# Gate projections of a hybrid decoder layer: eight quarter products per pair of column blocks, or seven

## The chip, the cores and the metric

The kernel runs on one core of one Trainium2 chip. The metric is the device time of one execution in microseconds (us), median of several; lower is better. Everything is float32 at the borders of the kernel: inputs and the output.

Four engines matter here. TensorE (PE) multiplies and writes to PSUM. VectorE (DVE) and ScalarE (ACT) do elementwise work, and only they and PE reach PSUM. SyncE (SP) issues most DMA transfers, ACT and GpSimd (POOL) a few. Each engine works through its own list of instructions in order and waits where an operand, or the buffer for a result, isn't ready.

## What is computed

One layer of a decoder on 256 tokens with 2048 channels, cut to what matters:

```python
h = rms_norm(x, g_pre)
proj = h @ w_in                       # 2048 -> 17424 columns, 8192 of them are g_logits
(a_val, a_gate, sq, sk, sv, s_gate, cq, ck, cv, c_gate, c_lr, mq, m_gate, g_logits) = split(proj)
y_a = pool_mixer(a_val, a_gate, w_pool, pool_scale)          # causal pooling, 1024 wide
y_b = swa_mixer(sq, sk, sv, s_gate)                          # window attention, 512 wide
y_c = gla_mixer(cq, ck, cv, c_lr, c_gate, ...)               # gated linear attention, 1024 wide
y_m = mem_attn(mq, m_gate, mem, g_mem, w_mem_kv)             # attention into 256 memory tokens, 512 wide
gates = sigmoid(g_logits.reshape(B, S, 4, 2048) + b_merge)
merged = (gates[:, :, 0] * (y_a @ w_br_pool) + gates[:, :, 1] * (y_b @ w_br_swa)
          + gates[:, :, 2] * (y_c @ w_br_gla) + gates[:, :, 3] * (y_m @ w_br_mem))
out = x + rms_norm(merged @ w_out, g_post)
```

The gate projection is `h` (256 x 2048) times 16 blocks of weights (2048 x 512), one block for each branch `b` (0 pooling, 1 window, 2 linear, 3 memory) and each quarter `j` of the channels.

## The kernel before

**Precision by splitting.** Every large operand is split into a high and a low part in the format float32r, which PE multiplies in one pass: `hi = round(x)`, `lo = x - hi`. A product takes three matmuls: hi by hi, hi by lo, lo by hi. A weight unit of 1 MB comes into one of three `raw` buffers by an SP transfer (`load_raw`, L104). `split_w` (L110) then makes two halves of 1024 columns: ACT copies to `hi` (L113) and DVE subtracts (L114). There are five pairs of `hi` and `lo` buffers.

**Two forms of product.** `a_block` (L117) has the activations stationary and 512 weight columns moving: for each of its k slices of 128 channels and for both token tiles t, three matmuls (L133, L134, L135) into one of four PSUM banks of the tag `acc`. `b_unit` (L146) has the weights stationary and both parts of the activations moving: 16 times a matmul of 512 columns (L156) and one of 256 (L157), then a sum (L161, L162) and an `evac` function that multiplies by the row of 1/rms. The activations `h_at` are x times `g_pre`; 1/rms is applied behind each product, as a column (`xscol`) or a row (`xsrow`).

**Background work.** The small chains of the four mixers are generators in `queue`; `pull` takes one step of them between weight units. A scheduler then orders each engine's list, so that neighbours can swap; the tables of buffers set who waits for whom.

**Stages.** First x is loaded and split while the values `sv` of the window attention are computed (three `a_block`s from L278), then come the `b_unit`s of the window attention (28), the memory branch (12) and the linear attention (16), and then `merge` (L438) for each branch: memory, window, linear, and pooling last. `merge` computes for each quarter j the gate block (`a_block` over 16 slices, evacuated by L447 on DVE and the tanh of L448 on ACT into a tile of the tag `c2`), and behind it the branch projection (`a_block` over 4 or 8 slices), which L453, L455 and L456 multiply by the gate and add to `merged`. The pooling units (`av`, `ag`, 16) stand between the gates of memory and linear attention. The last `merge` also transposes `merged` (`transpose_block`, L695), and the output projection (`o0` to `o4`, L733 to L753), a norm and the residual follow.

The pieces at which the prediction looks are the branch ends, such as this one of before:

```python
                    vec.scalar_tensor_tensor(gates[t][:], gates[t][:], 1.0, a, op0=ALU.add, op1=ALU.mult)
                    vec.tensor_tensor(merged[t][:, js], merged[t][:, js], gates[t][:], op=ALU.add)
```

## Time and profile before

| what | value |
|---|---|
| time, median of 3 runs | 1184.74 us (1184.65 to 1184.75) |
| span of the profiled execution | 1182.7 us |
| between the span and the median | 2.0 us |
| PE, DVE, ACT, POOL busy | 1172.6, 715.9, 555.3, 13.8 us |
| granted TensorE clock, all stages | 1.00 |
| moved by DMA | 230.44 MB, mean 195 GB/s |
| first 8 us, 8 to 74 us: PE busy | 5.89, 65.78 us |
| 1170 us to the end: PE busy | 4.96 of 13.0 us |

The profiled execution has no time of its own beside its span; the 2.0 us to the median of the runs are what lies around it. A row of the timeline gives start, duration, engine, line, operation, output and inputs, and in brackets the idle time before it with its releaser. Durations of instructions on one engine overlap: the next one starts before the last one's results have landed. So what an instruction costs a full engine is the distance between two starts, and its duration is what a follower waits that needs the result.

### The profile page before, as it was taken

To read this page: it belongs to the slowest core of one execution; us is meant where nothing else is said; L and a number is where in the kernel's file an instruction comes from. 1 tells how busy PE (TensorE), PEld (TensorE's weight loads), DVE (VectorE), ACT (ScalarE), POOL (GpSimd) and SP (SyncE) were. 2 spreads that over 40 slices of the span, in tenths; PEclk is the share of its full clock that TensorE was granted. 3 is DMA by queue.
4 is the path that set the end of the run, shared out by engine and by line. 5 is a ranking of instruction groups with operands and counts; after the bars stand their busy time and mean duration, and the time that the engine had idled before them with its cause. 6 is when DMAs were issued, how large, how long until landed. Compare 5 with 4: busy or idle time off the path is not lost.

```text
span 1182.7 us, 15065 instructions
## 1 busy us (share of the span) xinstructions
PE 1172.6 (99%) x6014; PEld 1001.8 (85%) x6014; DVE 715.9 (61%) x943; ACT 555.3 (47%) x734; POOL 13.8 (1%) x36
## 2 busy tenths in 40 slices
PE   9999999999999999999999999999999999999997
PEld 7888888888888888899888888888888888888887
DVE  6656665664665555545856666777655555656454
ACT  7656444444554444345644444454444444444441
POOL 0000000000000000000000000000000000000000
PEclk9999999999999999999999999999999999999999
DMA  9867544544445555356444455555555555556642
GB/s 354 324 226 260 178 147 175 178 148 174 178 169 192 200 199 201 133 185 221 178 163 176 156 184 199 179 186 194 214 193 205 204 189 205 193 187 241 257 145 105
DMA packets 38838, 230.44 MB, mean 195 GB/s; under 512 B 4448, under 2 KB 4832, under 8 KB 14832
## 3 DMA queue, kind: packets, MB, share of 16 engines
q1 hardware_dynamic: 38048, 228.28, 54.5%
q10 hardware_dynamic: 720, 1.21, 0.3%
q8 instruction: 47, 0.77, 0.3%
q14 instruction: 23, 0.19, 0.0%
HBM read 227.37 MB, written 2.10 MB: 194 GB/s over the span
## 4 chain that ended last, share of the span: by engine, by line
PE 98%; issue 0%; DMA 0%; DVE 0%; ACT 0%; SPq 0%; DVEq 0%; POOLq 0%; POOL 0%
PE sp L341 1%; PE gmem0a L133 1%; PE gmem2a L133 1%; PE gmem1a L133 1%; PE gswa0a L135 1%; PE gmem2a L135 1%; PE gswa0a L133 1%; PE gmem0a L135 1%; PE gmem1a L135 1%; PE vma L135 1%; PE gmem2a L134 1%; PE gmem0a L134 1%; PE gpool1a L135 1%; PE o0a L135 1%; PE gmem1a L134 1%; PE vma L133 1%
## 5 line engine op out<-in xcount | busy, mean ns | idle before, releaser
L306 ACT ACTIVATE th<-xg 128x256 f32<-128x256 f32 x24 | 9.9, 411 | 18.1 <-DVE xg L304 18.1
L344 DVE SCALAR_TENSOR_TENSOR s<-big_cst,sp 128x128 f32<-128x128 f32 (+1 forms) x24 | 7.3, 349 | 3.5 <-PE sp L341 3.5
L341 PE MATMUL sp<-k,q 128*128 128x128 f32 (+1 forms) x48 | 9.1, 326 | 0.0
L349 ACT ACTIVATE s<-s,st 128x384 f32<-128x384 f32 (+1 forms) x8 | 6.2, 775 | 4.8 <-DVE st L348 4.8
L341 PEld LDWEIGHTS sp<-k,q 128*128 128x128 f32 x48 | 7.3, 190 | 0.8
L578 POOL TENSOR_TENSOR sq<-sq 128x256 f32<-128x256 f32 x4 | 3.4, 854 | 384.5 <-ACT sq L577 360.4
L179 ACT ACTIVATE xhl<-xr,vecs 128x256 fp32r<-128x256 f32 x16 | 6.9, 499 | 1.9 <-DMA xr<-in_xT 1.2
L704 ACT ACTIVATE mTh<-mtp 128x512 fp32r<-128x512 f32 x8 | 4.3, 596 | 6.5 <-PE mtp L702 6.5
L180 DVE SCALAR_TENSOR_TENSOR xhl<-xr,vecs,xhl 128x256 fp32r<-128x256 f32 x16 | 6.8, 482 | 0.7 <-ACT xhl L179 0.6
L367 PE MATMUL po<-pt,sv 128*128 128x256 f32 x24 | 7.2, 380 | 0.0
L179 ACT ACTIVATE mhl<-mr,vecs 128x256 fp32r<-128x256 f32 x16 | 7.0, 495 | 0.0
L180 DVE SCALAR_TENSOR_TENSOR mhl<-mr,vecs,mhl 128x256 fp32r<-128x256 f32 x16 | 6.9, 479 | 0.0
L759 DVE SCALAR_TENSOR_TENSOR yg<-yg,opart,xres 128x640 f32<-128x640 f32 (+2 forms) x8 | 5.5, 748 | 1.3 <-POOL opart L756 1.3
L348 DVE TENSOR_REDUCE st<-s 128x1 f32<-128x384 f32 (+1 forms) x8 | 6.0, 748 | 0.1
L726 ACT ACTIVATE oj<-o4a 128x256 f32<-128x256 f32 x2 | 0.8, 383 | 10.6 <-PE o4a L753 10.6
L362 ACT ACTIVATE pt<-tp 128x384 f32<-128x384 f32 x12 | 5.7, 477 | 0.0
L705 DVE SCALAR_TENSOR_TENSOR mTl<-mtp,mTh 128x512 fp32r<-128x512 f32 x8 | 5.2, 686 | 0.7 <-ACT mTh L704 0.4
L322 DVE TENSOR_TENSOR sqh<-sq,sqh 128x256 fp32r<-128x256 f32 x4 | 1.7, 424 | 5.9 <-ACT sqh L321 5.9
L456 DVE TENSOR_TENSOR merged<-merged,gmem 128x512 f32<-128x512 f32 x8 | 5.1, 684 | 0.0
L456 DVE TENSOR_TENSOR merged<-merged,ggla 128x512 f32<-128x512 f32 x8 | 5.1, 684 | 0.0
L456 DVE TENSOR_TENSOR merged<-merged,gpool 128x512 f32<-128x512 f32 x8 | 5.1, 684 | 0.0
L368 PEld LDWEIGHTS po<-pt,sv 128*128 128x128 f32 x24 | 4.6, 190 | 0.6
(3495 smaller groups left out, 4397.0 us busy)
## 6 DMA issues: line engine op xcount, KB each, us to landing
raw<-in_w_g SPq DMA_DIRECT2D x64, 1024.0 KB, 4.8
raw<-in_w_sqk SPq DMA_DIRECT2D x24, 1024.0 KB, 4.9
raw<-in_w_out SPq DMA_DIRECT2D x12, 1024.0 KB, 4.8
raw<-in_w_sv SPq DMA_DIRECT2D x8, 1024.0 KB, 7.7
raw<-in_w_cqk SPq DMA_DIRECT2D x8, 1024.0 KB, 4.8
raw<-in_w_cg SPq DMA_DIRECT2D x8, 1024.0 KB, 4.9
raw<-in_w_av SPq DMA_DIRECT2D x8, 1024.0 KB, 4.8
raw<-in_w_ag SPq DMA_DIRECT2D x8, 1024.0 KB, 4.9
```

The source lines that it names most:

```text
L133: ten.matmul(o, lhsT=sh[:, ts], rhs=hi[:, ws], start=(k == 0), stop=False)
L134: ten.matmul(o, lhsT=sh[:, ts], rhs=lo[:, ws], start=False, stop=False)
L135: ten.matmul(o, lhsT=sl[:, ts], rhs=hi[:, ws], start=False, stop=(k == nk - 1))
L179: act.activation(h, rawx[:, i, :], AF.Copy, scale=g[:, k : k + 1])
L180: vec.scalar_tensor_tensor(l, rawx[:, i, :], g[:, k : k + 1], h.bitcast(F32), op0=ALU.mult, op1=ALU.subtract)
L306: act.activation(th[:], xg[:], AF.Tanh, scale=0.5)
L341: ten.matmul(parts[g], lhsT=q3[:, g, it * P : (it + 1) * P], rhs=k3[:, g, :nj], start=True, stop=True)
L344: vec.scalar_tensor_tensor(s[:, g, :], dist[:, g, :], SLOPES[g * 4 + hh], parts[g], op0=ALU.mult, op1=ALU.add)
L348: vec.tensor_reduce(st[:, 0:1], s[:], axis=AX.XY, op=ALU.max, negate=True)
L349: act.activation(s[:], s[:], AF.Exp, bias=st[:, 0:1], accum_out=st[:, 1:2])
L367: ten.matmul(po[:], lhsT=sv[g][:, 0, vs], rhs=pt[g][:, 0:T], start=(g == 0), stop=False)
L456: vec.tensor_tensor(merged[t][:, js], merged[t][:, js], gates[t][:], op=ALU.add)
```

## The change

The gate projections are computed with seven quarter products instead of eight. For a pair of neighbouring column blocks j0, j1 of one branch, `h` is cut into four quarters (two token tiles by two halves of the channels) and the two weight blocks into four (two halves of the channels by two blocks). Sums and differences of quarters are multiplied in seven products instead of eight and put together again. The sums of activations (`quarter`, made once) are split into hi and lo; those of the weights are made on DVE for each of eight slices `kk` (L420, L421, L426) and split afterwards. The bias enters by a small matmul (`bias`).

For this, `h` is now normalised before it is split (`x_prep`), so that no product needs the 1/rms any more, and the memory branch's values `vm` are computed first, while x is prepared. The gates are no longer computed in `merge`: a generator `all_gates` is drawn on by `gates(work)`, which every `b_unit` and `a_block` calls with the PE time of the piece just issued; each step of the generator costs so much of a credit (0.8 for a half of a plain weight unit, 6.6 for a slice `kk` with sums). The finished gates (32 tiles of 128x512) are written to DRAM by ACT's queue and read back by SP's when the branch projections run, all of them at the end, quarter by quarter. The outputs of linear attention and pooling also wait in DRAM, over POOL's queue. PSUM is divided anew: the tag `seven` has four banks, `acc` two instead of four, `sm` two instead of four.

```diff
+GATE_SHARE = 1.07
...
     def sm(name, shape):
-        return ps.tile(shape, F32, tag="sm", bufs=4, name=name)
+        return ps.tile(shape, F32, tag="sm", bufs=2, name=name)
 
     def acc(name, shape):
-        return ps.tile(shape, F32, tag="acc", bufs=4, name=name)
+        return ps.tile(shape, F32, tag="acc", bufs=2, name=name)
+
+    def seven(name):
+        return ps.tile([P, 512], F32, tag="seven", bufs=4, name=name)
...
+    def gates(work):
+        if gate_stream[0] is None:
+            return
+        credit[0] += GATE_SHARE * work
+        while credit[0] > 0 and gate_stream[0] is not None:
+            try:
+                credit[0] -= next(gate_stream[0])
+            except StopIteration:
+                gate_stream[0] = None
...
+    def x_prep():
+        for c in range(4):
+            xn.append(c4(f"xn{c}", [P, 4, T]))
+            sync.dma_start(xn[c][:], ins["xT"][:, 4 * c : 4 * c + 4, :])
+            squares(xsq, xn[c], c)
+            for i in range(4):
+                k = 4 * c + i
+                act.activation(xn[c][:, i, :], xn[c][:, i, :], AF.Copy, scale=g_pre[:, k : k + 1])
+            yield
+        fold(xsq)
+        pr = sm("xpr", [P, T])
+        ten.matmul(pr[:], lhsT=ones[:], rhs=xsq[:, 0, 0], start=True, stop=True)
+        pool.memset(xsq[:, 1, 1], -0.5)
+        inv_rms(xrow, pr[:], xsq[:, 1, 1])
+        yield
+        for c in range(4):
+            for i in range(4):
+                vec.tensor_tensor(xn[c][:, i, :], xn[c][:, i, :], xrow, op=ALU.mult)
+            put_hilo(h_at.four(c, 0), h_at.four(c, 1), xn[c][:])
+            yield
...
+    def put_gate(b, j, t, src, dst):
+        act.activation(dst, src, AF.Tanh, scale=0.5)
+        gate_dram[b, j, t] = spill(f"gd{b}{j}{t}", [P, 512], F32)
+        act.dma_start(gate_dram[b, j, t][:], dst)
+
+    def gate_pair(b, jj):
+        j0, j1, n = 2 * jj, 2 * jj + 1, f"{b}{jj}"
+        w = ins["w_g"]
+        p1 = seven(f"p1{n}")
+        bias(p1[:], 4 * b + j0)
+        p1c = c2(f"p1c{n}", [P, 512])
+        for u in range(4):
+            raw = load_raw(w[b, j0, u], 2048)
+            for hf in range(2):
+                hi, lo = split_w(raw[:, hf * 1024 : (hf + 1) * 1024], 1024, f"gu{n}{u}{hf}")
+                for i in range(2):
+                    k = 4 * u + 2 * hf + i
+                    ws = slice(i * 512, (i + 1) * 512)
+                    mm3(p1[:], *tok(0, k), hi[:, ws], lo[:, ws], False, k % 8 == 7, k >= 8)
+                if u == 1 and hf == 1:
+                    act.activation(p1c[:], p1[:], AF.Copy)
+                yield 0.8
+        c11 = c2(f"c11{n}", [P, 512])
+        put_gate(b, j0, 0, p1[:], c11[:])
+        q4, q5, q6, q7 = [seven(f"q{i}{n}") for i in (4, 5, 6, 7)]
+        bias(q5[:], 16 + 2 * b + jj)
+        for kk in range(8):
+            raw = new_raw()
+            r4 = raw[:].rearrange("p (j u c) -> p j u c", j=2, u=2)
+            u, cs = kk // 4, slice((kk % 4) * 512, (kk % 4 + 1) * 512)
+            for j in range(2):
+                sync.dma_start(r4[:, j], w[b, j0 + j, u : u + 3 : 2, :, cs].rearrange("u p c -> p u c"))
+            vec.tensor_tensor(r4[:, :, 0, :], r4[:, :, 0, :], r4[:, 1, :, :], op=ALU.add)
+            vec.tensor_tensor(r4[:, 1, 1, :], r4[:, 1, 1, :], r4[:, 0, 0, :], op=ALU.add)
+            hi, lo = split_w(raw[:, 1024:2048], 1024, f"gt{n}{kk}a")
+            st, sp = kk == 0, kk == 7
+            mm3(q7[:], *quart(2, kk), hi[:, 0:512], lo[:, 0:512], st, sp)
+            mm3(q6[:], *quart(1, kk), hi[:, 512:1024], lo[:, 512:1024], st, sp)
+            vec.tensor_tensor(r4[:, 0, 1, :], r4[:, 0, 1, :], r4[:, 1, 1, :], op=ALU.add)
+            hi, lo = split_w(raw[:, 0:1024], 1024, f"gt{n}{kk}b")
+            mm3(q5[:], *quart(0, kk), hi[:, 0:512], lo[:, 0:512], False, sp)
+            mm3(q4[:], *tok(1, kk + 8), hi[:, 512:1024], lo[:, 512:1024], st, sp)
+            yield 6.6
+        v3, c21 = c2(f"v3{n}", [P, 512]), c2(f"c21{n}", [P, 512])
+        vec.tensor_tensor(p1c[:], q6[:], p1c[:], op=ALU.subtract)
+        vec.tensor_tensor(v3[:], q7[:], p1c[:], op=ALU.add)
+        vec.tensor_tensor(c21[:], q4[:], v3[:], op=ALU.subtract)
+        put_gate(b, j0, 1, c21[:], c21[:])
+        vec.tensor_tensor(v3[:], q5[:], v3[:], op=ALU.add)
+        put_gate(b, j1, 1, v3[:], v3[:])
+        vec.tensor_tensor(q5[:], q5[:], p1c[:], op=ALU.add)
+        for u in range(2, 4):
...
+                    mm3(q5[:], *quart(3, kk), hi[:, ws], lo[:, ws], False, kk == 7, True)
+                yield 0.8
+        put_gate(b, j1, 0, q5[:], c12[:])
...
+    for j in range(4):
+        merged[j] = c4(f"merged{j}", [P, 2, 512])
+        for i, (name, b, at, nky) in enumerate(branches):
+            a_block(f"b{name}{j}", [ins[f"w_br_{name}"][j, u] for u in range(nky // 4)], at, 512, br_evac(i, b, j))()
+        transpose_block(j)
```

Below, a "gate step" is one slice `kk` (its tiles are named `gt`), a "unit" is a `b_unit`, and `gu` and `gv` are the halves of plain gate weights ahead of and behind the eight steps of a pair. There are 8 pairs, so 64 gate steps, 64 `gu` halves and 32 `gv` halves.

How this moves instructions is shown at three places. The first is ACT's list near the start. In before, three blocks of `sv` follow each other and ACT does little but split their weights (`sv130h` and so on) and square x for the norm:

```order
L113 ACTIVATE sv130h<-raw_445 128x1024
L113 ACTIVATE sv131h<-raw_445 128x1024
L209 ACTIVATE xsx_447,xsssq<-xsx_447 128x1024
L243 ACTIVATE sv_107<-sv0a_111,xscol 128x512
L243 ACTIVATE sv_107<-sv0a_112,xscol 128x512
L113 ACTIVATE sv200h<-raw_497 128x1024
L113 ACTIVATE sv201h<-raw_497 128x1024
```

In the changed kernel the first block is `vm`, whose last four splits (`vm30h` to `vm33h`) stand among the preparation of the last chunk of the memory (`mhl`, `msq`) and of all four chunks of x (`xsq` squares, `xn` scaled by `g_pre`):

```order
L246 ACTIVATE xsq<-xn_275 128x1024
L319 ACTIVATE xn_275<-xn_275,vecs 128x256 x4
L246 ACTIVATE xsq<-xn_293 128x1024
L265 ACTIVATE mhl_96<-mr_302,vecs 128x256
L319 ACTIVATE xn_293<-xn_293,vecs 128x256 x4
L265 ACTIVATE mhl_96<-mr_302,vecs 128x256 x3
L246 ACTIVATE msq<-mr_302 128x1024
L138 ACTIVATE vm30h<-raw_301 128x512
L246 ACTIVATE xsq<-xn_328 128x1024
L138 ACTIVATE vm31h<-raw_301 128x512
L319 ACTIVATE xn_328<-xn_328,vecs 128x256 x4
L138 ACTIVATE vm32h<-raw_301 128x512
```

What moved: the squares and the scaling of x, which ran behind or beside three blocks, now stand ahead of the end of the first.

The second place is DVE's list in the middle, while the window attention's units run. One gate step (`gt115`, the raw buffer raw_6120) stands between the units `sq22` and `sk22`:

```order
L139 TENSOR_TENSOR sq220l<-raw_6058,sq220h 128x1024
L420 TENSOR_TENSOR raw_6120<-raw_6120 128x2x512
L139 TENSOR_TENSOR sq221l<-raw_6058,sq221h 128x1024
L421 TENSOR_TENSOR raw_6120<-raw_6120 128x512
L426 TENSOR_TENSOR raw_6120<-raw_6120 128x512
L139 TENSOR_TENSOR gt115al<-raw_6120,gt115ah 128x1024
L139 TENSOR_TENSOR gt115bl<-raw_6120,gt115bh 128x1024
L139 TENSOR_TENSOR sk220l<-raw_6147,sk220h 128x1024
L201 SCALAR_TENSOR_TENSOR q_5728<-sq22a,sq22s 128x256
L139 TENSOR_TENSOR sk221l<-raw_6147,sk221h 128x1024
```

In before, DVE had only the two splits of each unit there, a sum and a product by the row of 1/rms; the three additions and two more splits per step are new, and the product is gone.

The third place is PE's list at the end of a branch projection. In before, the gates' block `ggla1` follows the linear attention's branch block `bgla0`, with other PSUM tiles:

```order
L133 MATMUL bgla0a_7159<-bgla011h,yc_3836 128x512
L134 MATMUL bgla0a_7159<-bgla011l,yc_3836 128x512
L135 MATMUL bgla0a_7159<-bgla011h,yc_3837 128x512
L133 MATMUL ggla1a_7239<-ggla100h,xhl_91 128x512
L134 MATMUL ggla1a_7239<-ggla100l,xhl_91 128x512
```

In the changed kernel the next branch block `bpool0` follows, and with two `acc` banks in all its two tiles take the banks of `bgla0`:

```order
L144 MATMUL bgla0a_8591<-bgla011h,yc_8492 128x512
L145 MATMUL bgla0a_8591<-bgla011l,yc_8492 128x512
L146 MATMUL bgla0a_8591<-bgla011h,yc_8492 128x512
L144 MATMUL bpool0a_8668<-bpool000h,ya_8495 128x512
L145 MATMUL bpool0a_8668<-bpool000l,ya_8495 128x512
```

What moved: nothing stands between the last matmul of one branch block and the first of the next, and the next one writes where DVE still reads.

More of the change, by code (lines that the diff above doesn't have):

```diff
@@ L229 @@
-    x_chunk, h_at = make_T("x", ins["xT"], g_pre)
-    col, row, x_rstd = make_rstd("xs", ins["x"])
-    m_chunk, m_at = make_T("m", ins["memT"], g_mem)
-    mcol, mrow, m_rstd = make_rstd("ms", ins["mem"])
-    def run(gen):
-        for _ in gen:
-            pass
-    sv = [c4(f"sv{g}", [P, 2, 512]) for g in range(3)]
-    def sv_evac(j):
-        def evac(t, a):
-            act.activation(sv[j][:, t, :], a, AF.Copy, scale=col[:, t : t + 1])
-        return evac
-    first_x = x_chunk.load(0)
+        at.four = lambda c, i: hl[c][:, :, i, :]
@@ new lines, with m_put, m_norm @@
+    m_at = hilo_tiles("m")
+    msq = e8("msq", [P, 2, 4, T])
+    mrow = msq[:, 1, 0]
+    mcol = cst.tile([P, 2], F32, name="mcol")
+    def m_put(rawx, c, i):
+        k = 4 * c + i
+        h, l = m_at(k)
+        act.activation(h, rawx[:, i, :], AF.Copy, scale=g_mem[:, k : k + 1])
+        vec.scalar_tensor_tensor(l, rawx[:, i, :], g_mem[:, k : k + 1], h.bitcast(F32), op0=ALU.mult, op1=ALU.subtract)
+    def m_norm():
+        fold(msq)
+        pr = sm("mpr", [P, T])
+        ten.matmul(pr[:], lhsT=ones[:], rhs=msq[:, 0, 0], start=True, stop=True)
+        pc = sm("mpc", [P, 2, 2])
+        for t in range(2):
+            ten.matmul(pc[:, t, :], lhsT=msq[:, 0, 0, t * P : (t + 1) * P], rhs=ones[:, 0:2], start=True, stop=True)
+        pool.memset(msq[:, 1, 1], -0.5)
+        inv_rms(mrow, pr[:], msq[:, 1, 1])
+        inv_rms(mcol[:], pc[:, :, 0], half[:])
@@ L262, in load_first @@
         for i in range(4):
-            x_chunk.put(first_x, 0, i)
-        return raw
-    def mem_prep():
-        for c in range(4):
-            yield from m_chunk(c)
-        yield from m_rstd()
-    x_rstd_steps = x_rstd()
-    def load_second(u, src):
-        raw = load_raw(src, 2048)
-        next(x_rstd_steps)
-        return raw
-    sv_done = a_block("sv0", [ins["w_sv"][0, u] for u in range(4)], h_at, 512, sv_evac(0), load_first,
-                      lambda u: 1)
-    sv_done1 = a_block("sv1", [ins["w_sv"][1, u] for u in range(4)], h_at, 512, sv_evac(1), load_second)
@@ new lines, in quart, with tok, bias_prep @@
+    def quart(i, kk):
+        return quarter[i][:, 0, kk, :], quarter[i][:, 1, kk, :]
+    def tok(t, k):
+        sh, sl = h_at(k)
+        return sh[:, t * P : (t + 1) * P], sl[:, t * P : (t + 1) * P]
+    brow = cst.tile([48, 512], R, name="brow")
+    sel = cst.tile([48, 24], R, name="sel")
+    def bias_prep():
+        raw = c2("braw", [48, 512])
+        pool.memset(raw[:], 0.0)
+        rows = ins["b_merge"].rearrange("b (j c) -> (b j) c", c=512)
+        sync.dma_start(raw[0:16, :], rows)
+        sync.dma_start(raw[32:48, :], rows)
+        act.activation(brow[:], raw[:], AF.Copy)
+        vec.tensor_tensor(brow[32:48, :], raw[32:48, :], brow[32:48, :].bitcast(F32), op=ALU.subtract)
+        one = c2("bsel", [48, 24])
+        vec.tensor_tensor(one[:, 0:16], ident[0:48, 0:16], ident[0:48, 32:48], op=ALU.add)
+        two = one[:, 0:16].rearrange("p (r i) -> p r i", i=2)
+        vec.tensor_tensor(one[:, 16:24], two[:, :, 0], two[:, :, 1], op=ALU.add)
+        vec.tensor_copy(sel[:], one[:])
+        yield
@@ new lines, in bias @@
+    def bias(o, r):
+        ten.matmul(o, lhsT=sel[:, r : r + 1].to_broadcast([48, P]), rhs=brow[:], start=True, stop=False)
+    gate_dram = {}
+    def put_gate(b, j, t, src, dst):
[24 more added lines that the diff above has]
+        for kk in range(8):
+            raw = new_raw()
+            r4 = raw[:].rearrange("p (j u c) -> p j u c", j=2, u=2)
[22 more added lines that the diff above has]
+        for u in range(2, 4):
+            raw = load_raw(w[b, j1, u], 2048)
+            for hf in range(2):
+                hi, lo = split_w(raw[:, hf * 1024 : (hf + 1) * 1024], 1024, f"gv{n}{u}{hf}")
+                for i in range(2):
+                    kk = 4 * (u - 2) + 2 * hf + i
+                    ws = slice(i * 512, (i + 1) * 512)
+                    mm3(q5[:], *quart(3, kk), hi[:, ws], lo[:, ws], False, kk == 7, True)
+                yield 0.8
+        c12 = c2(f"c12{n}", [P, 512])
+        put_gate(b, j1, 0, q5[:], c12[:])
@@ L288, with all_gates @@
+    def all_gates():
+        for jj in range(2):
+            for b in range(4):
+                yield from gate_pair(b, jj)
+    queue.append(("quarters", bias_prep()))
+    queue.append(("quarters", quarter_prep()))
+    vec.tensor_scalar(g_gla, g_gla, 0.5, None, op0=ALU.mult)
+    vec.tensor_scalar(p_scale, p_scale, 0.5, None, op0=ALU.mult)
+    walpha = cst.tile([16, 512], F32, name="walpha")
+    sync.dma_start(walpha[:], ins["w_alpha"])
     big_cst = cst.tile([P, 1344], F32, name="big_cst")
```

487 lines of the change are left out of this document (247 added, 240 removed).

## The prediction

> **What bounds the kernel now.** I read the page first: the busy shares, the slices, and the chain that ended last.
>
> ```profile
> span 1182.7 us, 15065 instructions
> PE 1172.6 (99%) x6014; PEld 1001.8 (85%) x6014; DVE 715.9 (61%) x943; ACT 555.3 (47%) x734; POOL 13.8 (1%) x36
> ...
> PE   9999999999999999999999999999999999999997
> ...
> DVE  6656665664665555545856666777655555656454
> ...
> GB/s 354 324 226 260 178 147 175 178 148 174 178 169 192 200 199 201 133 185 221 178 163 176 156 184 199 179 186 194 214 193 205 204 189 205 193 187 241 257 145 105
> ...
> PE 98%; issue 0%; DMA 0%; DVE 0%; ACT 0%; SPq 0%; DVEq 0%; POOLq 0%; POOL 0%
> ```
>
> PE is full in every slice but the last, and the chain is 98% PE. So each matmul removed is time gained, as long as PE does not wait in its place; each wait of PE is time lost. DVE stands at 61% and nowhere above 8 tenths, and the transfers reached 354 GB/s where they were asked to. Two windows (busy time of PE, PEld, DVE, ACT and POOL, then granted clock, DMA share, GB/s) show the stages that the change touches: weight units with background work, and gates with branch projections.
>
> ```profile
> 74.00:260.00 186.00, 186.00 (x1076) 162.85 (x1075) 118.53 (x187) 91.14 (x137) 0.70 (x1) 1.00 0.53 187
> 840.00:975.00 135.00, 135.00 (x603) 112.05 (x602) 78.59 (x80) 58.00 (x61) 0.00 (x0) 1.00 0.58 203
> ```
>
> PE has no idle time in either. DVE has 118.53 of 186.00 (64%) and 78.59 of 135.00 (58%): this spare time is what the change spends. The base of the sum is the span, 1182.7, and 2.0 around it, which gives the median of 1184.7.
>
> **What is removed: PE −39.9.** Each of 8 pairs takes 168 matmuls of 512 columns instead of 192, and two small bias matmuls are added, of 512 columns each: 22 fewer per pair, 176 in all. A full PE starts one every
>
> ```profile
> 700.09 0.39 PE L134 MATMUL gmem3a<-gmem300l,xhl 128*128 128x512 f32 x1
> ...
> 708.48 0.39 PE L135 MATMUL gmem3a<-gmem311h,xhl 128*128 128x512 f32 x1
> ...
> 499.76 0.28 PE L157 MATMUL ck3a<-xhl,ck30l 128*128 128x256 f32 x1
> ...
> 502.58 0.28 PE L157 MATMUL ck3a<-xhl,ck31l 128*128 128x256 f32 x1
> ```
>
> The first two rows are 37 matmuls apart: 8.39 / 37 = 0.2268 us, and 176 × 0.2268 = 39.9. The other two rows are 8 pairs of a unit apart, 2.82 / 8 = 0.3525, so a unit of 16 pairs takes 5.64 us of PE. This term is a count and a pitch; I give it no range.
>
> **The start: +8 (5 to 10).** In before PE starts with `sv0` at 5.88 and comes to its second block at 29.07. In the changed kernel ACT prepares memory and x ahead of the first block's end.
>
> ```profile
> 5.20 0.63 ACT L113 ACTIVATE sv000h<-raw_first 128x512 fp32r<-128x512 f32 x1 [1.48 <-DMA raw_first<-in_w_sv]
> ...
> 10.01 1.71 ACT L179 ACTIVATE xhl<-xr,vecs 128x256 fp32r<-128x256 f32 x4
> 11.63 0.62 ACT L113 ACTIVATE sv010h<-raw_first 128x512 fp32r<-128x512 f32 x1
> 12.15 0.62 ACT L113 ACTIVATE sv011h<-raw_first 128x512 fp32r<-128x512 f32 x1
> ```
> ```profile
> 5.88 0.73 PE L133 MATMUL sv0a<-sv000h,xhl 128*128 128x512 f32 x2 [0.93 <-ACT sv000h L113]
> ...
> 29.07 0.39 PE L133 MATMUL sv1a<-sv100h,xhl 128*128 128x512 f32 x1
> ```
> ```profile
> 571.36 1.05 ACT L113 ACTIVATE cg50h<-raw 128x1024 fp32r<-128x1024 f32 x1
> 572.31 1.04 ACT L113 ACTIVATE cg51h<-raw 128x1024 fp32r<-128x1024 f32 x1
> ```
>
> Four activations of 256 columns take 1.62 (10.01 to 11.63), a split of 512 takes 0.52, one pass over 1024 columns 0.95. A chunk of the memory with its weights then costs ACT 1.62 + 4 × 0.52 + 0.95 (the squares) = 4.65, four of them 18.6; a chunk of x costs 0.95 + 1.62 = 2.57, four 10.3. From 5.2 on that ends at 34 to 35, and the next block's first split comes a us later, its low part on DVE another 1.2: PE starts it at about 37.5, against 29.07 now. That is 8.4 late; I take 8. At best DVE and ACT share so that 5 are lost; at worst the transfers, which this stage asks for at 354 GB/s, add 2.
>
> The longest idle time of PE in before is the 0.93 in the row at 5.88, and both windows grant the clock 1.00, so no row shows what a long pause does. [...]
>
> **The branch projections: +12 (8 to 20), and +3 (0 to 6) for the first.** In before a gate block of other PSUM tiles follows each branch block.
>
> ```profile
> 853.68 0.39 PE L135 MATMUL bgla0a<-bgla011h,yc 128*128 128x512 f32 x1
> 853.69 1.28 DVE L455 SCALAR_TENSOR_TENSOR ggla<-ggla,bgla0a 128x512 f32<-128x512 f32 x2
> ...
> 853.91 0.39 PE L133 MATMUL ggla1a<-ggla100h,xhl 128*128 128x512 f32 x1
> ```
> ```profile
> 1107.34 0.39 PE L135 MATMUL o0a<-o031h,mTl 128*128 128x512 f32 x1
> 1107.76 0.60 ACT L726 ACTIVATE oj<-o0a 128x512 f32<-128x512 f32 x1 [0.98 <-PE o0a L135]
> 1108.24 0.39 PE L133 MATMUL o1a<-o100h,mTh 128*128 128x512 f32 x1
> 1108.54 1.32 DVE L727 TENSOR_TENSOR yg<-o0a,gpost 128x512 f32<-128x512 f32 x2 [0.50 <-ACT oj L726]
> ```
>
> Now the next block writes the bank that the first of the two L455 reads. It starts at 853.69 and, two of them taking 1.28, is read out at about 854.37; with 0.07 for the release the next block starts at 854.44 instead of 853.91: 0.53. There are 16 branch blocks, so 15 such ends make 8.0. The output projection loses two of four banks as well: the first `yg` product would be done at 1108.54 + 0.69 + 0.05 = 1109.28 while `o1` starts at 1108.24, so 1.04 at each of three ends and 0.8 at the small last one, about 4. Sum 12. Nothing covers it, since both banks belong to one block. It could be 8 if DVE and ACT stand ready at each end; 20 if DVE is in the middle of a split of 1.22 at half of the 16 (8 × 1).
>
> The very first block needs gates read back from memory. Their loads stand in SP's list behind a weight load that waits for a buffer; that is one buffer's turn late. One transfer takes 4.8 from issue to landing:
>
> ```profile
> raw<-in_w_g SPq DMA_DIRECT2D x64, 1024.0 KB, 4.8
> ```
>
> I take 3; 0 if the bank is not needed before, 6 if a whole transfer and a split stand between.
>
> **The stage with the gates: +10 (3 to 40).** Here the cost hides in DVE's spare time, or does not.
>
> ```profile
> 578.87 1.22 DVE L114 TENSOR_TENSOR cg51l<-raw,cg51h 128x1024 fp32r<-128x1024 f32 x1
> 580.00 1.22 DVE L114 TENSOR_TENSOR cg60l<-raw,cg60h 128x1024 fp32r<-128x1024 f32 x1
> 581.14 0.42 DVE L162 TENSOR_TENSOR cg4s<-cg4a,cg4s 128x256 f32<-128x256 f32 x1
> 581.47 1.22 DVE L114 TENSOR_TENSOR cg61l<-raw,cg61h 128x1024 fp32r<-128x1024 f32 x1
> ```
> ```profile
> 786.22 0.69 DVE L639 TENSOR_TENSOR win<-u 128x512 f32<-128x512 f32 x1
> 787.02 0.69 DVE L639 TENSOR_TENSOR win<-win 128x512 f32<-128x512 f32 x1
> 787.63 1.22 DVE L114 TENSOR_TENSOR av300l<-raw,av300h 128x1024 fp32r<-128x1024 f32 x1
> ```
>
> Starts lie 1.13 apart for 1024 columns (578.87 to 580.00), 0.33 for a sum of 256, 0.61 for an addition of 512 (787.02 to 787.63). A result is free 0.11 after the duration (786.22 + 0.69 to 787.02). A gate step is a chain: the addition of 1024, 1.22 + 0.11 = 1.33; the addition of 512 and ACT's split behind it, 0.69 + 0.11 + 1.05 = 1.85, in which L426 fits; two low parts, 2.26. Together 5.44. A unit now costs DVE 2 × 1.13 + 0.33 = 2.6. The credit lets about 1.09 units pass per step: DVE 5.44 + 1.09 × 2.6 = 8.27, PE 12 × 0.2268 + 1.09 × 5.64 = 8.87. So 0.6 us per step is left for the mixers' own chains and for waits.
>
> Over the whole stage: PE has 1360 gate matmuls at 0.2268 (308), the 64 units from `ck0` on at 5.64 (361), some 480 matmuls of the value blocks (110) and small pieces, for which I put 50: about 830. DVE has 64 × 5.44 = 348, 96 halves of plain gate weights × 1.13 = 108, 64 units × 2.6 = 166, the value blocks 46, the ends of pairs 32, and background: the first window's 118.53 holds 30 units, each with two splits of 1.22 and two operations of 0.42, which leaves 20 per 186 us, or some 88. That is 788 of 830, 95%. It fits, with little to spare. Where it is uneven, PE waits: at the borders of `gu` and `gv` halves, where several units stand between two steps. With these durations for every instruction of the two lists, DVE has 27.7 against PE's 25.2 around `gv10` and `gu20`, and 26.6 against 23.8 around `gv21` and `gu31`; what the buffers of split weights don't absorb of such borders is about 5.5 in all. And in five of eight pairs `q7` begins right behind the last `gu` matmul and needs the bank that ACT must empty: 0.42 (1107.34 to 1107.76) + 0.60 + 0.05 − 0.23 = 0.84 each, 4.2. Together 10. At best 3, if background chains move aside; at worst 40, if the steps' chain sets the pace (the rival B). The gates' weights are read as 14 MB per pair instead of 8. A `gu` block of 1 MB feeds 12 matmuls, 2.7 us, and the credit lets 1.5 us of units (0.27 MB) pass beside it: 1.27 MB in 4.2 us, 316 GB/s, below the 354 of the first slice. A ring of three buffers gives each 4.2 / 1.27 × 3 = 10 us, where 4.8 for landing and about 4 for waiting, splitting and release need 9. I cost that at nothing while landing stays below 6. The moved stores and reads of finished gates, 16.8 MB, go over the ACT and SP queues; ACT's list stands at 49% (91.14 of 186.00), so 32 issues like the one below are hidden there.
>
> ```profile
> 0.73 0.41 ACTq L85 DMA_DIRECT2D vecs<-in_vecs  x1
> ```
>
> **The sum:** 1184.7 − 39.9 + 8 + 12 + 3 + 10 = **1178** (1177.8). The low ends give 1184.7 − 39.9 + 5 + 8 + 0 + 3 = 1161, the high ends 1221.
>
> **The rivals.** *A*, the forecast: about 1178, chance 0.41, its own range 1168 to 1186.
>
> *B, slower than before*: DVE's chain becomes the bound of each gate step. Its place is L420 to the second low part of `gt`. For it speaks the 95% above, and that ACT's split of 1.05 in the middle waits in a list behind units' splits; against it, that the scheduler can put a unit's split into the chain's gaps, where pure DVE work is only 4.6. It decides from a step that takes 0.2 us more than PE has (12 / 64 more than my 10 brings the time back to before). With another split of 1.13 caught inside the chain of two steps in three, 0.53 beyond the margin of 0.6, 64 × 0.35 = 22 are lost, and 2 at each of 8 borders of pairs, less the 10 already counted: 1178 + 22 + 16 − 10 = 1206. Chance 0.28. [...]
>
> *C, the cover holds*: the start costs 5, branch ends 8, gates 3, the first branch 1.5: about 1162. For it: no window of before has PE waiting although DVE is at 64%. Chance 0.20.
>
> *D, transfers*: landing goes from 4.8 to 7 where the gate loads add 75% and stores come in; then a buffer's turn of 9 becomes 11.2 where 10 are there, 12% of the `gu` phases (32 × 4.2 = 134), so 16 in all, 1194. Against it: 354 GB/s in the first slice, more than the 316 asked for. Chance 0.09. That the change does not do what it says (the gates not finished before the branch projections, so that a rest of the stream runs bare) gets 0.02: 5 us per step left over, 1183 for one.
>
> **How the numbers follow.** Two kernels of this length can be told apart at 0.2%, so same is 1182.4 to 1187.1. Faster: C 0.20, most of A (0.35), and a part of D and B 0.05, together 0.60. Same: the top of A and the low part of B, 0.12. Slower: B and D beyond, 0.28. The range for 8 in 10 leaves out 0.08 below and 0.12 above: 1160 to 1208. The likeliest is 1178.
>
> **What would show it.** The changed profile should have 176 fewer matmuls of 512 columns and PE busy about 1135. At the start, PE idle between 24 and 38 with ACT as releaser, and `km0` first at 37.5. At each branch end, about 0.5 idle of PE ended by DVE's product of gate and `acc` bank; three ends of about 1.0 in the output projection. In the gate stage, DVE above 9 tenths in the slices and PE idle of about 10 with releasers `gt…l` (DVE) and `p1` (ACT); under B these are several times that, under D the releaser is the DMA of `raw`, under C PE idle in this stage is below 4. I am wrong if PE's pitch of 0.2268 is not kept where DVE and transfers run fuller, or if a gate step's chain overlaps with the next one's, so that DVE's spare time does not matter at all.

## The result and the profile after

The changed kernel takes 1404.99 us (median of 4, 1402.30 to 1409.81) where before takes 1184.74: a ratio of 1.186, 95% interval 1.184 to 1.189. The forecast was 1178. The page of the changed kernel, the lines that answer to those of before:

```profile
span 1403.8 us, 15468 instructions
...
PE 1207.4 (86%) x5842; PEld 990.4 (71%) x5842; DVE 970.2 (69%) x1198; ACT 645.7 (46%) x843; POOL 108.6 (8%) x52
...
PE   7104998798999999899988999998988968999997
...
DVE  7113766567987876887877798787678855666544
...
PEclk9556999999999999999999999999999979999999
...
PE 12%; DVE 2%; issue 1%; DMA 1%; ACT 1%; DVEq 0%; POOLq 0%; POOL 0%; SPq 0%; ACTq 0%
```

PE has fewer matmuls than before (5842 records, 6014 before) and yet more busy time: 1207.4, where 1172.6 − 39.9 = 1132.7 would be left if they followed each other as before. It is also idle for 1403.8 − 1207.4 = 196 us instead of 10. (The last line, the chain, adds up to 17% of the span only and names rows of the end, so it doesn't tell where the time went.) A second line stands out: POOL, at 13.8 us before, has 108.6. The windows of the changed kernel (busy time of PE, PEld, DVE, ACT and POOL, then granted clock, DMA share, GB/s) are cut at the first matmuls of `km0a`, `ck0a`, `bmem0a` and `o0a`:

```profile
0.00:124.90 124.90, 31.56 (x124) 24.86 (x124) 35.19 (x63) 36.34 (x65) 86.15 (x14) 0.64 0.29 107
124.90:172.40 47.50, 47.50 (x256) 41.14 (x257) 37.55 (x52) 26.17 (x34) 1.54 (x3) 0.95 0.43 158
172.40:1146.90 974.50, 892.94 (x4365) 732.53 (x4363) 746.00 (x905) 488.78 (x637) 16.55 (x28) 0.97 0.64 228
1146.90:1302.30 155.40, 144.76 (x613) 114.15 (x613) 102.64 (x124) 58.47 (x60) 3.19 (x6) 0.96 0.72 257
1302.30:1403.80 101.50, 90.67 (x488) 77.72 (x488) 48.84 (x57) 35.97 (x50) 1.13 (x2) 0.98 0.42 145
```

PE is idle for 93 us in the first stretch, 82 in the stretch with the gates, 11 and 11 in the branch projections and the output. The last two are near the size that was forecast; the first two are not. The first stretch is told by POOL's timeline, of the changed kernel

```profile
38.07 42.09 POOL L255 TENSOR_TENSOR xsq<-xsq 128x256 f32<-128x256 f32 x1 [4.94 <-DVE xsq L254]
82.04 41.42 POOL L255 TENSOR_TENSOR msq<-msq 128x256 f32<-128x256 f32 x1 [1.88 <-DVE mcol L254]
123.43 0.70 POOL L255 TENSOR_TENSOR mcol<-mcol,half 128x2 f32<-128x2 f32 x1
```

and of before:

```profile
40.17 0.71 POOL L213 TENSOR_TENSOR xscol<-xsmean,half 128x2 f32<-128x2 f32 x1 [38.27 <-DVE xsmean L212]
```

It is the power of −1/2 for 1/rms. Before takes it of a column (2 elements per partition, 0.71 us) and spreads that to a row by a matmul; the changed kernel takes it of whole rows of 256 elements, at 42 us each, one behind the other. PE's row shows the price:

```profile
124.90 0.79 PE L185 MATMUL km0a<-mhl,km00h 128*128 128x512 f32 x1 [85.49 <-ACT vm L284]
```

The chain of causes is `km0a` for a PSUM bank of `vma`, ACT's evacuation of that for `mcol`, and `mcol` for POOL. The bank is a link of its own: `acc` has two banks now, and `vma` holds both. Whether `km` would have gone on with the four of before is not shown by a run.

For the stretch with the gates I read one turn of a gate step in the window attention's units, in three timelines of the changed kernel. SP, which issues the loads:

```profile
723.13 0.88 SPq L419 DMA_DIRECT2D raw<-in_w_g  x2
724.26 0.34 SPq L132 DMA_DIRECT2D raw<-in_w_sqk  x1
734.31 0.88 SPq L419 DMA_DIRECT2D raw<-in_w_g  x2
```

DVE, which adds and splits:

```profile
721.88 1.22 DVE L139 TENSOR_TENSOR gt014bl<-raw,gt014bh 128x1024 fp32r<-128x1024 f32 x1
723.02 1.22 DVE L139 TENSOR_TENSOR sq101l<-raw,sq101h 128x1024 fp32r<-128x1024 f32 x1
...
728.79 1.23 DVE L420 TENSOR_TENSOR raw<-raw 128x1024 f32<-128x1024 f32 x1 [0.65 <-DMA raw<-in_w_g]
...
733.06 1.22 DVE L139 TENSOR_TENSOR gt015bl<-raw,gt015bh 128x1024 fp32r<-128x1024 f32 x1
734.20 1.22 DVE L139 TENSOR_TENSOR sk101l<-raw,sk101h 128x1024 fp32r<-128x1024 f32 x1
```

PE, which waits:

```profile
731.94 0.73 PE L144 MATMUL q<-gt015ah,quarter 128*128 128x512 f32 x2 [2.10 <-ACT gt015ah L138]
```

The load of step `gt015` is issued at 723.13, just as DVE ends `gt014bl` (721.88 + 1.22 = 723.10): it takes the buffer of the step before. The other two buffers are held by units, whose halves stand on either side of a step (`sq101l` behind `gt014bl`, `sk101l` behind `gt015bl`). (Here a new tile got the buffer that came free first in the program's order, not the one that had been filled first.) The data come at 728.8, the chain ends at 734.28, and the next load leaves at 734.31. The turn is 11.2 us, where a step and a unit give PE 2.72 + 5.64 = 8.4. DVE itself waits for the data (0.65) and is not full.

This turn is no single case. Of the 64 first additions of a step, 34 found DVE waiting for the load; their row on the page of the changed kernel, with the idle time before them and what ended it:

```profile
L420 DVE TENSOR_TENSOR raw<-raw 128x1024 f32<-128x1024 f32 x64 | 78.8, 1231 | 61.9 <-DMA raw<-in_w_g 61.7
```

### The profile page after: what moved, and what is told of

It reads as the page before. It is cut to its first block, busy times and chain, and to the rows that moved or that the text cites. A ratio compares the mean times of both kernels' runs of the same rounds, so it can differ in the third digit from the quotient of the medians.

```text
span 1403.8 us, 15468 instructions
## 1 busy us (share of the span) xinstructions
PE 1207.4 (86%) x5842; PEld 990.4 (71%) x5842; DVE 970.2 (69%) x1198; ACT 645.7 (46%) x843; POOL 108.6 (8%) x52
## 5 line engine op out<-in xcount | busy, mean ns | idle before, releaser
L420 DVE TENSOR_TENSOR raw<-raw 128x1024 f32<-128x1024 f32 x64 | 78.8, 1231 | 61.9 <-DMA raw<-in_w_g 61.7
L185 PE MATMUL km0a<-mhl,km00h 128*128 128x512 f32 x8 | 5.1, 637 | 85.5 <-ACT vm L284 85.5
L421 DVE TENSOR_TENSOR raw<-raw 128x512 f32<-128x512 f32 x64 | 44.6, 697 | 1.3
L426 DVE TENSOR_TENSOR raw<-raw 128x512 f32<-128x512 f32 x64 | 44.2, 690 | 1.6
L255 POOL TENSOR_TENSOR xsq<-xsq 128x256 f32<-128x256 f32 x1 | 42.1, 42095 | 4.9 <-DVE xsq L254 4.9
L255 POOL TENSOR_TENSOR msq<-msq 128x256 f32<-128x256 f32 x1 | 41.4, 41418 | 1.9 <-DVE mcol L254 1.9
L329 DVE TENSOR_TENSOR xn<-xn,xsq 128x256 f32<-128x256 f32 x16 | 6.2, 449 | 41.2 <-POOL xsq L255 41.2
L228 DVE TENSOR_TENSOR xhl<-xn,xhl 128x1024 fp32r<-128x1024 f32 x4 | 4.9, 1221 | 41.5 <-ACT xhl L227 41.5
L843 DVE TENSOR_TENSOR merged<-merged,g 128x512 f32<-128x512 f32 x24 | 15.4, 684 | 0.0
L387 ACT ACTIVATE c<-q 128x512 f32<-128x512 f32 x8 | 4.8, 596 | 10.5 <-PE q L146 10.5
L592 POOL TENSOR_TENSOR ms<-ms,half 128x2 f32<-128x2 f32 x4 | 5.6, 1402 | 36.6 <-DVE ms L591 36.6
```

Of the source, the lines that this page charges most:

```text
L185: ten.matmul(a[:], lhsT=hi[:, ws], rhs=mov.both(k), start=(k == 0), stop=False)
L255: pool.tensor_tensor(dst, dst, exponent, op=ALU.pow)
L387: act.activation(dst, src, AF.Tanh, scale=0.5)
L420: vec.tensor_tensor(r4[:, :, 0, :], r4[:, :, 0, :], r4[:, 1, :, :], op=ALU.add)
L421: vec.tensor_tensor(r4[:, 1, 1, :], r4[:, 1, 1, :], r4[:, 0, 0, :], op=ALU.add)
L426: vec.tensor_tensor(r4[:, 0, 1, :], r4[:, 0, 1, :], r4[:, 1, 1, :], op=ALU.add)
```

## The experiments

A theory R came out of these rows: in the gate stage the hold on raw buffers sets the pace. Theory C is the forecast's rival B: DVE's chain sets it. Theory P: POOL's powers hold the start. The times stand against before, whose medians beside them are 1184.6 to 1185.6.

**1. The power on a column.** The base of most that follows:

```diff
...
-        pool.tensor_tensor(dst, dst, exponent, op=ALU.pow)
...
+        pool.tensor_tensor(col[:], col[:], half[:], op=ALU.pow)
+        for t in range(2):
+            vec.tensor_scalar(sq[:, 1, 1, t * P : (t + 1) * P], ident[:], col[:, t : t + 1], None, op0=ALU.mult)
...
+        ten.matmul(pr[:], lhsT=ones[:], rhs=sq[:, 1, 1], start=True, stop=True)
...
```

> The power of -1/2 for x and for the memory is taken on a column of 128x2 and spread to a row by a diagonal and a matmul with ones; nothing else changes. Theory P (the two powers over 128x256 on POOL, 42.09 and 41.42 us, hold PE for 85.5 us): 85 to 95 us less, about 1310 to 1320, with PE's pause ahead of km0a below 8 us and the clock there back at 1.00 in the third window of 50 us. Rival (the start waits for transfers or for ACT anyway): less than 40 us gained.

1326.87 us, 78.1 less, where 85 to 95 were expected. `km0a` starts at 43.9, 81.0 earlier; the stretch up to `ck0a` became 3.5 longer (51.0). Theory P holds; a little less came back than the pause had cost.

**2. Four raw buffers, and its control.**

```diff
-NB_HILO = 5
-NB_RAW = 3
+NB_HILO = 4
+NB_RAW = 4
```

> As e1_column_pow, with four raw buffers instead of three and four pairs of hi and lo instead of five (the same memory). Theory R (in the gate stage a load can be issued only when DVE has finished with an old raw buffer, and PE waits for the ring of three): PE's idle time between ck0a and bmem0a falls from about 81 to under 40, time 40 to 80 below e1_column_pow. Theory C (DVE's chain of additions and splits sets the pace of a step): within 10 us of e3_raw3_hilo4.

> As e1_column_pow with four pairs of hi and lo, and three raw buffers as there: the control for e2_raw4_hilo4. Theory R: 0 to 15 us slower than e1_column_pow. Theory C: 15 us or more slower, since split weights wait for PE to free a pair.

1233.91 with four buffers, 1334.91 for the control with only the pairs reduced: 101 us for one buffer. Against e1_column_pow it is 93 less, more than the 40 to 80 that I gave R. The gate stage in windows, first of e1_column_pow, then of e2_raw4_hilo4:

```profile
95.00:1067.30 972.30, 892.43 (x4364) 731.58 (x4362) 745.41 (x905) 489.68 (x637) 18.76 (x28) 0.97 0.65 228
```
```profile
91.10:972.30 881.20, 857.15 (x4364) 721.23 (x4362) 743.77 (x906) 501.65 (x638) 15.51 (x28) 0.99 0.71 252
```

DVE does the same work (745 and 744 us), PE's idle time falls from 80 to 24. DVE's own wait for the loads falls too, from 60.9 in e1_column_pow to 19.0 here:

```profile
L418 DVE TENSOR_TENSOR raw<-raw 128x1024 f32<-128x1024 f32 x64 | 78.1, 1221 | 19.0 <-DMA raw<-in_w_g 18.9
```

That speaks for R and against C: DVE could do its chain in the shorter time all along.

**3. No sums.** The three additions L420, L421 and L426 are taken out, so that a product takes plain quarters.

> As e1_column_pow; the three additions of a gate step (L420, L421, L426) are left out, so that the products are taken of plain quarters. Theory C: a step's chain on DVE falls from 5.4 to 2.3 us plus ACT's split, PE's idle time in the gate stage nearly goes (below 15), 100 us or more below e1_column_pow. Theory R: a raw buffer is held about 2.7 us less per step, but a landing of 5 us and the splits stay in the ring: 30 to 70 us less, PE still idle for 25 or more.

1228.42, 98 less than e1_column_pow. (Without the sums the gates come out different.) That is nearly the number that I expected of C, and more than the 30 to 70 of R; PE's idle time in the gate stage, 20.0, lies between what I gave the two. R can give such a gain, since the additions stand between a load's landing and the release of its buffer and so lengthen the hold, but I had put that too low. The run alone doesn't tell the theories apart. Run 2 does.

**4. One load per step.** Whole blocks in rows of 8 KB, so that other quarters are multiplied.

```diff
-            for j in range(2):
-                sync.dma_start(r4[:, j], w[b, j0 + j, u : u + 3 : 2, :, cs].rearrange("u p c -> p u c"))
+            sync.dma_start(raw[:], w[b, j0 + kk // 4, kk % 4])
```

> As e1_column_pow; each gate step fetches its 1 MB with one transfer of a whole block in rows of 8 KB, in place of two transfers in rows of 2 KB (so that other quarters of the weights are multiplied). Rival S (the small rows and the second issue make the loads late): PE's idle time in the gate stage falls by 30 us or more, time 1290 or less. Theory R (a load's issue waits for a free raw buffer, whatever its form): within 12 us of e1_column_pow's 1326.9.

1304.53, 22 less: between the two expectations. PE's idle time in the gate stage falls from 79.9 to 68.7 only. The second issue and the small rows are a part of what each turn costs, not the main one.

**5. The same three buffers, with the steps elsewhere.** This asks whether it is the number of buffers or how long units hold them.

```diff
             if hf == 0:
                 pull(1)
-                gates(2.8)
         evac(name, a)
         pull(1)
-        gates(2.8)
+        gates(5.6)
```

> As e1_column_pow (three raw buffers, five pairs of hi and lo); the gate stream is drawn once behind each weight unit instead of behind each of its two halves, so that no unit's raw buffer is held across a gate step. Theory R2 (two of the three buffers are held by units whose halves lie on both sides of a step, so each step's load waits for the step before, and a turn of one buffer, 5.6 us of landing and 5.6 us of chain, replaces PE's 8.4 to 8.9): PE's idle time in the gate stage falls to less than half, and the time to 1235 to 1280 from 1326.9. Theory R1 (three buffers are too few wherever the steps stand): within 25 us of e1_column_pow.

1241.18, 85.7 less than e1_column_pow; PE's idle time in the gate stage falls from 79.9 to 33.3. SP's list now sends loads of steps 8.5 and 8.6 us apart, here in the window attention's units:

```profile
673.50 0.88 SPq L416 DMA_DIRECT2D raw<-in_w_g  x2
678.99 0.34 SPq L132 DMA_DIRECT2D raw<-in_w_sqk  x1
682.03 0.95 SPq L416 DMA_DIRECT2D raw<-in_w_g  x2
687.35 0.34 SPq L132 DMA_DIRECT2D raw<-in_w_sqk  x1
690.67 0.88 SPq L416 DMA_DIRECT2D raw<-in_w_g  x2
```

DVE in the same stretch:

```profile
680.75 1.22 DVE L139 TENSOR_TENSOR sq201l<-raw,sq201h 128x1024 fp32r<-128x1024 f32 x1
...
686.10 1.22 DVE L139 TENSOR_TENSOR gt111bl<-raw,gt111bh 128x1024 fp32r<-128x1024 f32 x1
```

The load at 682.03 leaves as a unit gives its buffer back (680.75 + 1.22 = 681.97), 5.3 before DVE is done with the step before (`gt111bl`, 687.32). That unit was loaded at 669.62 and held its buffer for 12.4 us; in the changed kernel the unit loaded at 713.07 held one to the end of `sk101l`, 735.42, which is 22.4. It is the hold across a step (R2): three buffers were nearly enough, as long as a unit's two halves are not parted by one.

**6. Banks, share and start, each on e2_raw4_hilo4.** In e6 the branch and output blocks take `acc` and `seven` in turn, in e7 GATE_SHARE is 1.15, in e8 `x_prep` starts at `u == 3`.

```diff
+    def bank(name):
+        if late[0] == 0:
+            return acc(name, [P, 512])
+        late[0] += 1
+        return acc(name, [P, 512]) if late[0] // 2 % 3 == 0 else seven(name)
...
-        accs = [acc(f"{name}a{t}", [P, 512]) for t in range(2)]
+        accs = [bank(f"{name}a{t}") for t in range(2)]
...
```

> As e2_raw4_hilo4; after the gates, the branch and output blocks take the four banks of the tag seven and the two of acc in turn. The pauses of PE between branch blocks (0.38 each, 15) and between output blocks (0.82, 4) should go: 5.7 + 3.1 = 9 less, so 1225 against 1233.9. If DVE or the weights bound this stage instead, nothing changes. The pauses ahead of bmem0a and bswa0a stay.

> As e2_raw4_hilo4 with GATE_SHARE 1.15 in place of 1.07, so that the stream of gates ends some 5 units earlier. Theory T (the end of the stage costs because the last pair's end and the reload of gates stand bare): the pauses of 3.97 ahead of gv3120, 4.42 ahead of bmem0a and 4.13 ahead of bswa0a shrink, and the half clock behind them; 10 to 18 less, about 1220. Rival: the denser steps make DVE late in the middle of the stage, and the time rises by 5 or more.

> As e2_raw4_hilo4; the preparation of x starts with the last chunk of the memory's block instead of the third. If ACT's squares and scalings ahead of the splits of vm30 make the pause of 5.28 there, that pause falls below 2 and ck0a starts 3 to 6 us earlier than 91.1. Rival: the work is only moved behind km, and ck0a starts no earlier.

1217.67, 1220.61 and 1226.72: 16, 13 and 7 less than 1233.91. The two runs of e2_raw4_hilo4, e7 and e8 lie 5 us apart each, so the 7 of e8 are weakly known. In e8 `ck0a` starts at 86.8 instead of 91.1, as expected. Of e6 the branch stage is the sharpest reading of what two banks cost. Window of e2_raw4_hilo4, then of e6_more_banks, from `bmem0a` to `o0a`:

```profile
972.30:1127.90 155.60, 144.57 (x613) 114.26 (x613) 101.63 (x123) 57.56 (x59) 3.22 (x6) 0.96 0.73 255
```
```profile
979.80:1118.30 138.50, 138.18 (x613) 113.77 (x614) 100.23 (x121) 56.94 (x58) 3.02 (x5) 0.98 0.79 281
```

17 us in this stage and 4.4 in the output (101.5 to 97.1), where 9 were expected for both; the pause ahead of `bmem0a`, outside these windows, became longer by 2.6 in exchange.

**7. All together.** e9b_all has the three edits of 6, and the first two branch blocks ahead of the drain of the pooling chain; e9c lays the weights of the steps out a second time for one load each; e11 adds the edit of 5.

> e2_raw4_hilo4 with the edits of e6, e7 and e8 together, and the first two branch blocks ahead of the end of the pooling chain. If their gains add up, 1233.9 - 16 - 13 - 7 = 1198, and 5 less where the pauses ahead of bmem0a and bswa0a go as well; 1205 or more if they share a cause.

> As e9b_all, with the weights of the gate steps laid out a second time, so that each step is fetched by one transfer in rows of 8 KB. If loads are still late with four buffers, 5 to 15 below e9b_all; if the fourth buffer has covered them, within 4.

> As e9c_all_one_load, with the stream drawn once behind each unit as in e10. Theory R2: little more to gain with four buffers, within 8 of e9c_all_one_load; it is faster than before (below 1182) only if PE's idle time between ck0a and the first branch falls below 10.

1200.95, 1200.02 and 1209.93. The gains of 6 nearly add up. The new order of the first blocks brought nothing in time: the pauses ahead of `bmem0a` and `bswa0a` are gone, but PE waits 3.71 ahead of `mx` and 6.76 ahead of `bpool0a` instead. With the fourth buffer, one load per step is worth nothing that can be told. Moving the stream behind the units makes this version 10 slower, where I expected less than 8 either way: 9 of it lie in the gate stage (870.5 instead of 861.2 us, PE idle for 15.2 instead of 9.9), and the cause stays open.

**8. Are 176 matmuls worth 39.9?** They are added again, to the mended kernel and to the changed one; a product is accumulated several times, so that the gates differ.

```diff
+            for _ in range(3 if kk < 6 else 2):
+                ten.matmul(q5[:], lhsT=quart(0, kk)[0], rhs=hi[:, 0:512], start=False, stop=False)
```

> As e9c_all_one_load with 176 matmuls of 512 columns added (22 per pair, a product accumulated several times, so that the gates differ). If PE sets the pace of the mended kernel, 36 to 42 more (176 x 0.2268 = 39.9), about 1239; if DVE or loads set it, less than 20 more.

> The changed kernel itself with the same 176 matmuls added. Theory R (in the gate steps PE waits for loads that wait for buffers): a good part falls into PE's pauses, 10 to 28 more than 1405. If the pauses were beside the point, 40 more.

In the mended kernel 1231.99, 32.0 more than e9c_all_one_load. The windows from `ck0a` to `bmem0a`, of e9c_all_one_load and of e13_mended_plus176:

```profile
86.50:947.70 861.20, 851.31 (x4365) 717.66 (x4364) 742.39 (x901) 505.04 (x635) 13.49 (x26) 1.00 0.72 258
```
```profile
86.50:985.50 899.00, 889.95 (x4541) 750.87 (x4540) 744.25 (x901) 507.64 (x635) 14.13 (x26) 1.00 0.68 247
```

The total is below the 36 to 42 expected. 37.8 of the 39.9 are in this stage; some 5 come back in the branch stage (144.7 us from `bmem0a` to `o0a` in place of 149.8), where the pause ahead of `bpool0a` falls from 5.58 to 1.58. In the changed kernel 1406.57 (1400.78 and 1412.36), where 10 to 28 more were expected: 176 matmuls more cost nothing that can be told there, and PE's idle time in the gate stage falls from 81.6 to 54.8. So as many matmuls as the change removes were worth nothing in the kernel as it stood, not even the expected part.

**9. What was left.** e12 puts the pooling branch of the first two quarters behind the other three branches of both. e15 lets DVE add to `q5` one place earlier at a pair's end:

```diff
-        vec.tensor_tensor(c21[:], q4[:], v3[:], op=ALU.subtract)
-        put_gate(b, j0, 1, c21[:], c21[:])
-        vec.tensor_tensor(v3[:], q5[:], v3[:], op=ALU.add)
-        put_gate(b, j1, 1, v3[:], v3[:])
+        vec.tensor_tensor(c21[:], q5[:], v3[:], op=ALU.add)
         vec.tensor_tensor(q5[:], q5[:], p1c[:], op=ALU.add)
+        vec.tensor_tensor(v3[:], q4[:], v3[:], op=ALU.subtract)
+        put_gate(b, j1, 1, c21[:], c21[:])
+        put_gate(b, j0, 1, v3[:], v3[:])
```

e16 starts `x_prep` behind the memory's norm, e17 sets GATE_SHARE to 1.11, both on e15.

> As e9c_all_one_load; the pooling branch of the first two quarters comes behind the other three branches of both, so that the last pooling chain and its way through memory lie beside PE's work. The pauses of 3.64 (mx) and 5.58 (bpool0a) there and the half clock behind them go: 8 to 13 less, 1187 to 1192. If another transfer or DVE then holds the stage, within 4 of 1200.0.

> As e12_pool_later; at the end of a pair DVE adds to q5, for which PE's gv halves wait, one place earlier (the two gates of the second token tile change their order). The pauses of 0.88 and 2.47 ahead of gv3020 and gv3120 shrink by 0.7 each; 1 to 4 less than 1183.7. If the pauses come from the start of the chain rather than its length, nothing changes.

> As e15_q5_first; the preparation of x begins behind the memory's norm instead of beside the last chunk of vm. The pauses of 1.73 and 2.55 ahead of km0a and the half clock behind them go, 3 to 6 less; against that cq0a may wait for x, which ACT and DVE then prepare beside km alone (22 us of PE): with a wait of 5 or more there the time rises.

> As e15_q5_first with GATE_SHARE 1.11 in place of 1.15: the gates end later, steps stand less densely. If DVE's density costs PE's pauses in the middle, 2 to 5 less; if the tail costs, 2 to 8 more.

e12: 1183.74, 16 less than e9c_all_one_load, and level with before (0.9996, interval 0.9986 to 1.0005); e15: 1177.59, ratio 0.9934 (0.9920 to 0.9948), 0.7% below before and thus faster than both kernels; e16: 1183.73; e17: 1183.52. In e15 the pause ahead of `gv3020` went from 0.88 to 0.43 and the one of 2.47 ahead of `gv3120` went, with 0.46 ahead of `gv3121` in its place; the gain of 6 is more than I gave it, and more than these pauses. In e16 the pauses of 1.73 and 2.55 ahead of `km0a` became one of 3.35, and new ones came of 2.71 ahead of the norm's `xpr` and of 5.15 ahead of `cq0a`, which waits for x: the mishap named in its expectation. In e17 the pause ahead of `gv3120` is back, at 3.73: the tail costs. The page of e15_q5_first:

```profile
span 1176.2 us, 15382 instructions
...
PE 1153.5 (98%) x5846; PEld 972.3 (83%) x5846; DVE 965.8 (82%) x1203; ACT 658.8 (56%) x843; POOL 23.7 (2%) x49
```

## Why the prediction was wrong

The lengths of the stretches in us, for the changed kernel and the mended e15. They differ by 227.6 in all:

| stretch | changed | e15_q5_first |
|---|---|---|
| to `km0a` | 124.9 | 36.3 |
| `km0a` to `ck0a` | 47.5 | 50.0 |
| `ck0a` to `bmem0a` (gates) | 974.5 | 857.9 |
| `bmem0a` to `o0a` (branches) | 155.4 | 134.9 |
| `o0a` to the end | 101.5 | 97.1 |

**PE −39.9.** The count and the pitch were right, and in a kernel where PE is full they hold (37.8 in the stage, 32.0 in all). The step "each matmul removed is time gained, as long as PE does not wait in its place" had the condition that failed: in the changed kernel PE waits, and as many matmuls are worth nothing (e14). That e15 stands at 1177.6, beside the forecast of 1178, is chance: its start, its banks and its steps are not those that the forecast priced.

**The start, +8.** The step that failed is the sum of ACT's list, "that ends at 34 to 35", taken as the whole path. ACT's last split of that block did stand at 33.77. But behind it comes the norm, and I put no price on POOL's power, though the change made it from 2 elements to 256 and the row of before (0.71 for 2) was there. The two rows of it cost 83.5 us, of which taking it on a column gave back 78.1. Nor did I see that `km0a` needs a bank that only the end of the norm frees. The forecast `km0a` at 37.5 is met in e15 (36.3), which also prepares x later; in e1 it was 43.9.

**The branch projections, +12 and +3.** For the banks the mechanism and the size were right: PE is idle for 0.38 at an end, and its start is 0.53 behind its pitch (1193.84 after 1193.08; 0.53 forecast); behind an output block it is 0.82 and 0.98 (1326.05 after 1324.84; 1.04 forecast). The 0.07 for the release, which no PE row of before shows, is 0.14 in the changed kernel (L842, 1193.02 + 0.68, to 1193.84). At the first two blocks PE waits 4.43, 1.06 and 4.01, 9.5 where I took 3. Only the 4.01 ahead of `bswa0a` are of the forecast kind: the gates' reads leave at 1154.39, behind a weight load of 1154.01. The 4.43 ahead of `bmem0a` are ACT's: the split `bmem000h` stands in its list at 1145.80, behind the pooling chain's `yat` of 1144.74. The stage is 17 us longer than with six banks (155.6 and 138.5 in runs 2 and 6), the lower clock behind the first pauses included (granted 0.96 and 0.98 over the stage; in the changed kernel 0.50 from 1149 to 1153 and from 1162 to 1166); against e15 this stage and the output cost 20.5 and 4.4, where 15 were forecast.

**The stage with the gates, +10.** Here the forecast failed in size and in place. I worked the ring of three buffers out for the `gu` phases only, and then "I cost that at nothing while landing stays below 6"; the steps got no price for their buffers. The gates' loads did land in about 5 us (4.9 and 5.1 on the page), and yet a turn of one buffer was 11.2 us, because units parted by a step held the other two and each load left late. What did rise above my limit of 6 were the loads of units, issued 1.1 us behind a step's:

```profile
raw<-in_w_sqk SPq DMA_DIRECT2D x24, 1024.0 KB, 6.6
```

This landing, the last figure, was 4.9 in before, and is 4.9 again with four buffers.

The stage is 974.5 long where the mended one is 857.9: 117 instead of 10. Rival D named the releaser that DVE's row shows, the DMA of `raw`, but for slow landing in the `gu` phases and with 16 us; that its turn is 11.2 too is chance. Rival B, the one I gave 0.28, did not decide by DVE's load: DVE had 746 us of work in 974.5, against the 788 I had summed, and does it in 857.9 in e15. But its chain is half of the turn (728.79 to 734.28), which fits that e4, which shortens it, gained about as much as a fourth buffer. B's threshold was also worked out wrongly: by the forecast's own sum 7 us more, 0.11 a step, bring the time back to before, not 12 and 0.2.

**The clock.** The sum had no term for it. Two pauses with one matmul between them and what follows, in PE's timeline of the changed kernel:

```profile
1128.74 0.79 PE L185 MATMUL ag31a<-xhl,ag311h 128*128 128x512 f32 x1 [4.71 <-ACT ag311h L138]
1131.80 0.80 PE L144 MATMUL q<-gv3120h,quarter 128*128 128x512 f32 x1 [2.27 <-DVE q L438]
1132.40 0.63 PE L145 MATMUL q<-gv3120l,quarter 128*128 128x512 f32 x1
1132.82 0.63 PE L146 MATMUL q<-gv3120h,quarter 128*128 128x512 f32 x1
1133.25 0.63 PE L144 MATMUL q<-gv3120h,quarter 128*128 128x512 f32 x1
```

The pitch, from one start to the next, is 0.43 instead of 0.2268, and the granted clock 0.50 from 1132 to 1136. A shorter pause that stands alone:

```profile
579.23 0.74 PE L144 MATMUL q<-gt301ah,quarter 128*128 128x512 f32 x2 [1.87 <-ACT gt301ah L138]
580.18 0.64 PE L144 MATMUL q<-gt301bh,quarter 128*128 128x512 f32 x1 [0.21 <-ACT gt301bh L138]
580.61 0.63 PE L144 MATMUL q<-gt301bh,xhl 128*128 128x512 f32 x1
```

126 single rows of 512 columns have a duration of 0.60 to 0.66 in the changed kernel, none in before: at least 126 × 0.2 = 25 us of the 220. That is a third of the 75 by which PE's busy time exceeds the 1132.7; the rest was not taken apart. The trace shows half the clock behind the 2.27 and behind a pause of 1.87. In before no wait of PE is longer than 1 us, so no row there gave a number for it; it belonged to every stage that can wait, as a term of open size.
